# Down projection of seven row blocks by a 21-product identity over three token blocks

## The chip, the cores and the metric

The kernel runs on one core of one Trainium2 chip. The metric is the device time of one execution in microseconds, the median of three runs. One execution has a hardware profile: the time of every instruction on each engine. The engines are PE (matmuls), DVE (VectorE, elementwise), ACT (ScalarE, activations and copies), POOL (GpSimd, here only issuing DMAs) and SP (SyncE, issuing DMAs).

## What is computed

One step of a hybrid encoder layer for 384 tokens (256 of a prompt, 128 of running streams), model width 2048: a mixer (pooling branch and state-space branch), and then the MLP, which the change concerns:

```
x1 = x + rmsnorm(mixer output)
h  = square(relu(rmsnorm(x1) @ w_up))      # 384 x 8192
y  = x1 + rmsnorm(h @ w_down)              # w_down: 8192 x 2048
```

All is float32. A float32 product is made of three matmuls on rounded parts: an operand a is split into a high part (rounded to the type fp32r) and a low part (the rest), and a.b is taken as ah.bh + ah.bl + al.bh.

## The kernel before

**The MLP's work.** The 384 tokens are three blocks of 128 (b = 0, 1, 2). The 8192 hidden rows are eight row blocks (c8 = 0 to 7) of 1024 rows, or eight tiles f8 of 128. The 2048 output columns are two halves (p = 0, 1) of 1024 columns, each two blocks of 512. Call a block product the product of 128 tokens x 256 hidden rows x 512 columns: two tiles of rows with three matmuls each, 6 matmuls. Plainly computed, a half of a row block has 3 x 4 x 2 = 24 of them.

An up unit (half a tile f: 8 of the 16 tiles of model width) is 24 matmuls of 384 columns. When a tile's second unit is done, `up_evict` (L1319) takes relu and the norm's factor out of PSUM on DVE (L1322), squares on ACT (L1323), and makes the high part on ACT (L1332) and the low part on DVE (L1333) for the token blocks that are needed plain.

`down_units` (L1359) does a half of a row block for row blocks 0 to 6 in 8 steps of two units each. Token blocks 0 and 1 with the two halves of the row block's rows and the two column blocks go by a 2 x 2 identity of 7 products (r = 0 to 6) of 12 matmuls; token block 2 is computed plainly (r = 7 and 8, 24 matmuls each). That makes 132 matmuls a half. The sums of token blocks are made in `token_sums` (L1307: five DVE sums, one ACT rounding L1316, one DVE subtraction L1317, twice a row block). The sums of weights are DVE additions of 2048 columns (L1367), four a half, each made at the end of the preparation of an earlier step. Each finished product is copied out of PSUM by ACT (L1383) into one of two buffers `ev` and added by a POOL-issued DMA to `acc_scr` in DRAM (L1387; L1385 for the first row block): 9 a half.

The last row block (`last_units`, L1513) is computed plainly, the nine sums per half are loaded back (`begin_last`), `merge` (L1446) makes seven DVE sums a half of them, and the norm and the residual follow.

**Order.** Each engine runs its instructions in the order in which the program issues them. `run` (L1279) walks the list of units: it asks for the weights of the unit 8 later (SP), issues the matmuls of unit i, and prepares unit i + 4: `split4` (L1269) makes the high part of 1024 weight columns on ACT and the low part on DVE (L77 and L78, or L1275 and L1276 for every fourth). There are four pairs of buffers, so ACT's rounding for unit i + 4 waits for the matmuls of unit i. A unit's `post` (relu and so on for an up unit, eviction for a down unit) comes ahead of that preparation for an up unit and behind it for a down unit. The list alternates two down units and one up unit of the next row block (L1578 to L1582).

Of the kernel before, what the change touches and what calls it, by code (L numbers as in the profile page):

```python
# [7 lines left out]
F32 = mybir.dt.float32  # L8
# [25 lines left out]
V_GPRE, V_GMLP, V_PSC, V_CW, V_CB, V_NRM, V_DSK, V_DTB, V_ALOG, V_END = 0, 16, 32, 48, 240, 288, 320, 352, 353, 384  # L34


def build(ctx, tc, io):
# [963 lines left out]
    acc_scr = [[dram.tile([P, 512], F32, name=f"acc_scr{p}_{i}") for i in range(9)] for p in range(2)]  # L1001
# [258 lines left out]
    t8 = pg.tile([P, 8, T], F32, name="t8")  # L1260
    sf = pg.tile([P, 4, 2, P], F32, name="sf")
    sh = pg.tile([P, 4, 4, P], F32R, name="sh")
    sl = pg.tile([P, 4, 4, P], F32R, name="sl")
    raws = ExitStack()
    pr = raws.enter_context(tc.tile_pool(name="phr", bufs=4, reuse_waits="tile"))
# [13 lines left out]
    def run(units, far=8):  # L1279
        n = len(units)  # L1280
        got, hl = [None] * n, [None] * n

        def fetch(i):
            if i < n and units[i][0]:
                got[i] = units[i][0]()

        def prep(i):
            if i < n:
                hl[i] = units[i][1](got[i])

        for i in range(far):
            fetch(i)
        for i in range(DEPTH):
            prep(i)
        for i, (_, _, mm, post, soon) in enumerate(units):
            fetch(i + far)
            mm(hl[i])
            if soon:
                post()
            prep(i + DEPTH)  # L1300
            if not soon:
                post()
            hl[i] = got[i] = None

    nothing = lambda *_: None

    def token_sums(k):  # L1307
        a11, a12 = t8[:, k, :P], t8[:, 4 + k.start : 4 + k.stop, :P]
        a21, a22 = t8[:, k, P:TP], t8[:, 4 + k.start : 4 + k.stop, P:TP]
        f = [sf[:, i, :, :] for i in range(4)]  # L1310
        v.tensor_tensor(f[0], a22, a21, ALU.subtract)
        v.tensor_tensor(f[3], a11, a12, ALU.subtract)
        v.tensor_tensor(f[3], f[3], f[0], ALU.add)
        v.tensor_tensor(f[2], a11, a21, ALU.subtract)
        v.scalar_tensor_tensor(out=f[1], in0=f[0], scalar=-1.0, in1=a11, op0=ALU.mult, op1=ALU.subtract)
        s.activation(sh[:, :, k, :], sf, AF.Copy)  # L1316
        v.tensor_tensor(sl[:, :, k, :], sf, sh[:, :, k, :].bitcast(F32), ALU.subtract)  # L1317

    def up_evict(f, ps):  # L1319
        f8 = f % 8  # L1320
        t = t8[:, f8, :]
        v.scalar_tensor_tensor(out=t, in0=ps, scalar=0.0, in1=r2, op0=ALU.max, op1=ALU.mult)  # L1322
        s.activation(t, t, AF.Square)  # L1323
        blocks = range(3) if f8 >= 4 else (0, 2)
        n = len(blocks)
        tag = f"{f8}_{f // 8 % 2}"
        h = pg.tile([P, n, P], F32R, tag=f"hh{tag}", name=f"hh{f}")
        l = pg.tile([P, n, P], F32R, tag=f"hl{tag}", name=f"hl{f}")
        tb = t.rearrange("p (b t) -> p b t", b=3)
        if n == 2:  # L1330
            tb = tb[:, 0:3:2, :]
        s.activation(h, tb, AF.Copy)  # L1332
        v.tensor_tensor(l, tb, h.bitcast(F32), ALU.subtract)  # L1333
        return {b: (h[:, i, :], l[:, i, :]) for i, b in enumerate(blocks)}

    def up_units(c8, hh, skip=0):
        out = []
        for f8 in range(skip, 8):
            f = c8 * 8 + f8
            ps = []  # L1340
            for q in range(2):

                def mm(hl, f=f, q=q, ps=ps):
                    if q == 0:
                        ps.append(mmtile(f"pj_up{f}")[:, :T])
                    half(ps[0], q, hl, xs2)

                def post(f=f, f8=f8, q=q, ps=ps):
                    if q:
                        hh.append(up_evict(f, ps[0]))  # L1350

                out.append(
                    (lambda f=f, q=q: wfetch(io["w_up"][f, q], f"up{f}_{q}"), lambda w: split4(*w), mm, post, True)
                )
        return out

    NAMES = ("11", "12", "22", "21")

    def down_units(c8, p, hh):  # L1359
        nm = f"{c8}_{p}"  # L1360
        tok = lambda k0, b: lambda k: hh[k0 + k][b]
        sums = lambda i: lambda k: [sh[:, i, k, :], sl[:, i, k, :]]
        raw, t2 = {}, []
        src = {n: io["w_down"][c8, p, i] for i, n in enumerate(NAMES)}

        def add(d, n):
            v.tensor_tensor(raw[d], raw[d], raw[n], ALU.add)  # L1367

        steps = [
            ("11", True, [(0, tok(0, 0)), (7, tok(0, 2))], nothing),  # L1370
            ("12", True, [(8, tok(0, 2))], lambda: add("11", "12")),
            ("21", True, [(1, tok(4, 0)), (7, tok(4, 2))], nothing),
            ("22", True, [(2, sums(3)), (8, tok(4, 2))], lambda: add("12", "22")),
            ("11", False, [(4, sums(0))], lambda: add("22", "11")),
            ("12", False, [(6, sums(2))], lambda: add("21", "22")),
            ("22", False, [(5, sums(1))], nothing),
            ("21", False, [(3, tok(4, 1))], nothing),
        ]
        begins, ends = {7: 0, 8: 1}, {7: 2, 8: 3}

        def evict(r, o):
            e = pg.tile([P, 512], F32, tag="ev", name=f"ev{nm}_{r}", bufs=2)
            s.copy(e, o)  # L1383
            if c8 == 0:
                gp.dma_start(acc_scr[p][r], e)  # L1385
            else:
                gp.dma_start(acc_scr[p][r], e, accum_op=ALU.add)  # L1387

        out = []
        for j, (kd, load, uses, then) in enumerate(steps):  # L1390
            outs = []
            for q in range(2):
                half_cols = slice(q * 1024, q * 1024 + 1024)

                def fetch(kd=kd, q=q, hc=half_cols):
                    if q == 0:
                        raw[kd] = pr.tile([P, 2048], F32, tag="raw", name=f"raw{nm}_{kd}")
                    sy.dma_start(raw[kd][:, hc], src[kd][:, hc])

                def prep(_, j=j, q=q, kd=kd, hc=half_cols, then=then):  # L1400
                    hl = split4(raw[kd][:, hc], f"wd{nm}_{j}_{q}")
                    if q:
                        then()
                    return hl

                def mm(hl, j=j, q=q, uses=uses, outs=outs):
                    if j == 0 and q == 0:
                        t2.extend(sstile(f"t2_{nm}_{i}") for i in range(2))
                    if q == 0:
                        outs += [t2[r - 7] if r >= 7 else mmtile(f"wd{nm}_{r}") for r, _ in uses]  # L1410
                    wh, wl = hl
                    for k2 in range(2):
                        k = q * 2 + k2
                        c = slice(k2 * 512, k2 * 512 + 512)
                        for (r, a), o in zip(uses, outs):
                            ah, al = a(k)
                            first = k == 0 and (r < 7 or begins[r] == j)
                            fin = k == 3 and (r < 7 or ends[r] == j)
                            te.matmul(o, ah, wh[:, c], start=first, stop=False)  # L1419
                            te.matmul(o, ah, wl[:, c], start=False, stop=False)  # L1420
                            te.matmul(o, al, wh[:, c], start=False, stop=fin)  # L1421

                def post(j=j, q=q, uses=uses, outs=outs):
                    if q == 0:
                        return
                    for (r, _), o in zip(uses, outs):
                        if r < 7 or ends[r] == j:
                            evict(r, o)
                    if p == 0 and j < 2:
                        token_sums(slice(2 * j, 2 * j + 2))  # L1430

                out.append((fetch if load else None, prep, mm, post, False))
        return out

    c8 = NC - 1
    ac, hacc, tail = [], [], {}

    def begin_last():
        raws.close()
        fin = ctx.enter_context(tc.tile_pool(name="fin", bufs=1, reuse_waits="tile"))  # L1440
        for p in range(2):
            ac.append([fin.tile([P, 512], F32, name=f"ac{p}_{i}") for i in range(9)])
            for i in range(9):
                gp.dma_start(ac[p][i], acc_scr[p][i])

    def merge(p):  # L1446
        a1, a2, a3, a4, a5, a6, a7 = ac[p][:7]
        v.tensor_tensor(a2, a1, a2, ALU.add)
# [122 lines left out]
    def first_mm(hl, mm=mm):  # L1571
        mm(hl)
        norm2()
        for i in range(2):
            hh0.append(up_evict(i, ps_up[i]))
# [143 lines left out]
```

## Time and profile before

| what | value |
|---|---|
| median of 3 runs | 2796.72 us (2796.18 to 2797.13) |
| span of the profiled execution | 2795.4 us (the page gives no other time of it) |
| PE busy | 2783.4 us |
| DVE busy | 1766.9 us |
| ACT busy | 1323.8 us |
| granted clock of PE, mean | 0.999 |

The span is the time from the first to the last instruction. Matmuls are pipelined, so that the durations of single ones overlap; their cadence is read from their starts. "Idle before" a group is the time that the engine stood still ahead of it, with what it waited for.

### The profile page before, as it was taken

The numbers are of one execution on the slowest core, as the hardware profiler recorded it, in microseconds if no ns is written. First come the engines' busy times: TensorE is split into PE (matmuls) and PEld (weight loads), VectorE is DVE, ScalarE is ACT, GpSimd is POOL, SyncE is SP. The second block draws the span as 40 slices with busy tenths as digits, with TensorE's granted clock in tenths as the row PEclk, the third lists the DMA queues.
The fourth block names the chain that finished last, engine by engine and source line by source line (L and its number), as shares of the span: only waits on it lengthen the run. The fifth ranks groups of instructions, "written<-read, shape, count | busy, mean of one in ns | idle before, by whom it ended". The sixth has DMA issues, their size and how long they took to land.

```text
span 2795.4 us, 40257 instructions
## 1 busy us (share of the span) xinstructions
PE 2783.4 (100%) x15964; PEld 2654.1 (95%) x15964; DVE 1766.9 (63%) x2217; ACT 1323.8 (47%) x2076; POOL 191.0 (7%) x295
## 2 busy tenths in 40 slices
PE   9999999999999999999999999999999999999998
PEld 9999999999999999999999988999999999999997
DVE  8774334567767767667643333666767667676766
ACT  6443223555555555554422223545555555555553
POOL 0000000000000000001000000000111111111111
PEclk9999999999999999999999999999999999999999
DMA  6444445556556556555744454445666566666656
GB/s 223 135 134 139 137 141 172 190 171 216 196 179 211 196 183 206 200 182 187 263 154 159 148 201 135 159 164 185 178 159 166 162 161 163 179 178 185 181 128 247
DMA packets 161468, 492.89 MB, mean 176 GB/s; under 512 B 20032, under 2 KB 43392, under 8 KB 156416
## 3 DMA queue, kind: packets, MB, share of 16 engines
q1 hardware_dynamic: 133008, 406.07, 43.4%
q0 software_dynamic: 28128, 84.24, 12.6%
q8 instruction: 125, 2.05, 0.3%
q14 instruction: 63, 0.52, 0.1%
q10 hardware_dynamic: 144, 0.01, 0.0%
HBM read 412.35 MB, written 77.89 MB: 175 GB/s over the span
## 4 chain that ended last, share of the span: by engine, by line
PE 90%; DVE 4%; issue 2%; ACT 2%; DMA 1%; SPq 0%; POOL 0%; DVEq 0%; ACTq 0%; POOLq 0%
PE pj_up L162 6%; PE pj_up L163 6%; PE pj_up L164 6%; PE pj_x L164 3%; PE pj_x L162 3%; PE pj_x L163 3%; PE wd L1419 3%; PE pj_sp L163 3%; PE wd L1421 3%; PE wd L1420 3%; PE pj_sp L164 3%; PE pj_sp L162 3%; PE pj_z L162 2%; PE pj_z L163 2%; PE pj_z L164 2%
## 5 line engine op out<-in xcount | busy, mean ns | idle before, releaser
L162 PE MATMUL pj_up<-x1h,wh_up 128*128 128x384 f32 x992 | 334.2, 337 | 0.0
L163 PE MATMUL pj_up<-x1l,wh_up 128*128 128x384 f32 x992 | 333.3, 336 | 0.0
L164 PE MATMUL pj_up<-x1h,wl_up 128*128 128x384 f32 x992 | 333.3, 336 | 0.0
L162 PE MATMUL pj_x<-xgh,wh_x 128*128 128x384 f32 x768 | 257.2, 335 | 0.0
L164 PE MATMUL pj_x<-xgh,wl_x 128*128 128x384 f32 x768 | 256.6, 334 | 0.0
L163 PE MATMUL pj_x<-xgl,wh_x 128*128 128x384 f32 x768 | 256.6, 334 | 0.0
L78 DVE TENSOR_TENSOR wl_wd<-raw,wh_wd 128x1024 fp32r<-128x1024 f32 x168 | 201.9, 1223 | 62.7 <-ACT wh_wd L77 61.2
L77 ACT ACTIVATE wh_wd<-raw 128x1024 fp32r<-128x1024 f32 x168 | 174.2, 1053 | 84.5 <-PE pj_up L163 42.1
L162 PEld LDWEIGHTS pj_up<-x1h,wh_up 128*128 128x128 f32 x992 | 186.5, 188 | 4.5
L163 PEld LDWEIGHTS pj_up<-x1l,wh_up 128*128 128x128 f32 x992 | 186.5, 188 | 4.5
L164 PEld LDWEIGHTS pj_up<-x1h,wl_up 128*128 128x128 f32 x992 | 186.5, 188 | 0.0
L164 PE MATMUL pj_z<-xgh,wl_z 128*128 128x384 f32 x512 | 171.1, 334 | 0.0
L162 PE MATMUL pj_z<-xgh,wh_z 128*128 128x384 f32 x512 | 171.1, 334 | 0.0
L163 PE MATMUL pj_z<-xgl,wh_z 128*128 128x384 f32 x512 | 171.1, 334 | 0.0
L162 PE MATMUL pj_sp<-abh,wh_sp 128*128 128x384 f32 x512 | 171.0, 334 | 0.0
L163 PE MATMUL pj_sp<-abl,wh_sp 128*128 128x384 f32 x512 | 171.0, 334 | 0.0
L164 PE MATMUL pj_sp<-abh,wl_sp 128*128 128x384 f32 x512 | 171.0, 334 | 0.0
L78 DVE TENSOR_TENSOR wl_sp<-w_sp,wh_sp 128x1024 fp32r<-128x1024 f32 x64 | 78.4, 1225 | 110.7 <-ACT wh_sp L77 110.7
L162 PEld LDWEIGHTS pj_x<-xgh,wh_x 128*128 128x128 f32 x768 | 144.2, 188 | 0.0
L163 PEld LDWEIGHTS pj_x<-xgl,wh_x 128*128 128x128 f32 x768 | 144.2, 188 | 0.0
L164 PEld LDWEIGHTS pj_x<-xgh,wl_x 128*128 128x128 f32 x768 | 144.2, 188 | 0.0
L78 DVE TENSOR_TENSOR wl_x<-w_x,wh_x 128x1024 fp32r<-128x1024 f32 x72 | 87.5, 1222 | 81.3 <-ACT wh_x L77 81.3
(392 smaller groups left out, 7087.3 us busy)
## 6 DMA issues: line engine op xcount, KB each, us to landing
w_up<-w_up SPq DMA_DIRECT2D x126, 512.0 KB, 4.5
raw<-w_down SPq DMA_DIRECT2D x112, 512.0 KB, 7.2
w_x<-w_in SPq DMA_DIRECT2D x96, 512.0 KB, 4.2
w_z<-w_in SPq DMA_DIRECT2D x64, 512.0 KB, 4.6
w_sp<-w_ssd SPq DMA_DIRECT2D x64, 512.0 KB, 5.0
acc_scr<-ev POOLq DMA_DIRECT2D x126, 256.0 KB, 4.4
w_ga<-w_in SPq DMA_DIRECT2D x32, 512.0 KB, 3.5
w_pp<-w_pp SPq DMA_DIRECT2D x32, 512.0 KB, 3.4
```

Source lines behind the costliest of these rows:

```text
L77: s.activation(h, w, AF.Copy)
L78: v.tensor_tensor(l, w, h.bitcast(F32), ALU.subtract)
L162: te.matmul(out, wh, xh, start=first, stop=False)
L163: te.matmul(out, wh, xl, start=False, stop=False)
L164: return te.matmul(out, wl, xh, start=False, stop=last)
L1419: te.matmul(o, ah, wh[:, c], start=first, stop=False)
L1420: te.matmul(o, ah, wl[:, c], start=False, stop=False)
L1421: te.matmul(o, al, wh[:, c], start=False, stop=fin)
```

## The change

Seven row blocks' down products are now made by one bilinear identity over all three token blocks, the four pairs of row tiles and the two column blocks: 21 block products a half, 6 matmuls each. It has three tables. `A_FORMS` says how 21 token forms are made from the 12 blocks of h (three token blocks by four pairs of tiles) with 20 sums of 256 columns: 14 forms need one sum, 3 need two, 4 need none. Every form is then rounded on ACT and subtracted on DVE. `B_UNITS` lists 15 units a half: the sums of weight blocks (1024 columns) made first, the buffer that is split, the blocks loaded, and the products (form, bank). `C_OPS` lists 14 sums a half that make six output blocks of the 12 banks at the end.

```
+B_UNITS = [([], 0, [(5, 0)], [(0, 0), (1, 1)]), ([(0, 1, -1, 0, 1)], 0, [(7, 1)], [(2, 1)]),
+ ([(2, 1, -1, 2, 1)], 2, [(3, 2)], [(3, 2)]), ([(2, 3, 1, 2, -1), (1, 2, 1, 1, -1)], 1, [(2, 3)], [(4, 3), (5, 0)]),
+ ([], 3, [], [(6, 4), (7, 5)]), ([(4, 0, 1, 4, 1)], 4, [(1, 4)], [(8, 2), (9, 5)]),
+ ([(4, 5, 1, 4, -1), (0, 0, 1, 4, 1)], 0, [(0, 5)], [(10, 3)]), ([], 5, [], [(11, 4)]), ([], 2, [], [(12, 6)]),
+ ([(0, 2, -1, 4, 1)], 0, [], [(13, 7)]), ([(2, 3, -1, 2, 1)], 2, [(6, 3)], [(14, 8)]), ([], 3, [], [(15, 9)]),
+ ([(3, 3, -1, 6, 1), (3, 4, 1, 3, 1)], 3, [(4, 6)], [(16, 8), (17, 10)]), ([], 6, [], [(18, 10), (19, 9)]),
+ ([], 4, [], [(20, 11)])]
+NBUF, NSTAGE, NC_, LOOK = 7, 5, 12, 5
```

In what follows d0 to d14 are these units of a half: d1, d2, d5, d9 and d10 make one weight sum, d3, d6 and d12 two; d0, d3, d4, d5, d12 and d13 have two products, the others one.

The sums stand directly ahead of the split in a unit's preparation, and the forms are made in a new step at the end of each iteration of `run`, three at most, of those whose old content has been multiplied for the last time in half 1 of the row block before (`freed`):

```
             if not soon:
                 post()
+            if forms:
+                forms_step()
...
+    def form(c, r, ops, src, sign):
+        for d, x, sx, y, sy in ops:
+            signed_sum(part(c, d), part(c, x), sx, part(c, y), sy)
+        a, h, l = part(c, src), fh[r], fl[r]
+        s.activation(h, a, AF.Copy, scale=float(sign))
+        if sign > 0:
+            v.tensor_tensor(l, a, h.bitcast(F32), ALU.subtract)
+        else:
+            v.scalar_tensor_tensor(out=l, in0=a, scalar=-1.0, in1=h.bitcast(F32), op0=ALU.mult, op1=ALU.subtract)
+
+    def forms_step():
+        for _ in range(3):
+            if forms and forms[0][1] < freed[0] and (forms[0][0], forms[0][2]) in hid:
+                c, r, _, ops, src, sign = forms.popleft()
+                form(c, r, ops, src, sign)
...
+            def prep(_, ops=ops, b=b, g=g):
+                raw_load(g + LOOK)
+                for d, x, sx, y, sy_ in ops:
+                    signed_sum(raw[d], raw[x], sx, raw[y], sy_)
+                return split4(raw[b], f"wd{g}")
...
+            def post(prods=prods, u=u):
+                if p and u == 0:
+                    forms_begin(c8 + 1)
+                for r, c in prods:
+                    if p:
+                        freed[0] = r + 1
+                    if c_last[c] == r:
+                        e = pg.tile([P, 512], F32, tag="ev", name=f"ev{c8}_{p}_{c}", bufs=2)
+                        s.copy(e, bank[c])
```

`signed_sum` is one DVE instruction. `up_evict` keeps only relu and square; the results stay in seven `hid` tiles of two row tiles each. PSUM is divided into 2 banks for up units and 6 for down units instead of 4 and 4. Weight blocks go into seven fixed buffers, asked for on SP in the preparation of the unit five earlier. Twelve banks a half instead of nine are evicted to `acc_scr`; the twelve of half 0 are loaded back after the last up unit, those of half 1 with the last row block.

Up units run ahead: 24 come first (12 more than before), then the halves take 4 and 12 up units among their 15 down units, the last two row blocks 4 and 8, and 2 and 6:

```
+    def spread(downs, ups):
+        out, n = [], 0
+        for u, d in enumerate(downs):
+            while n < len(ups) and (n + 0.5) * len(downs) <= u * len(ups):
+                out.append(ups[n])
+                n += 1
+            out.append(d)
+        return out + ups[n:]
...
+            n = (4, 12)[p] if c < NC - 3 else {0: 4, 1: 8, 2: 2, 3: 6}[(c - NC + 3) * 2 + p]
+            units += spread(down_units(c, p), take(min(n, left)))
```

The forms of the first row block are made three an iteration from the twelfth up unit on, with nothing to wait for. Those of the last row block are plain roundings of the 12 blocks.

More of the change, by code (lines that the diff above doesn't have):

```diff
@@ L1000, in build @@
     x1_scr = dram.tile([P, 3, DM], F32, name="x1_scr")
-    acc_scr = [[dram.tile([P, 512], F32, name=f"acc_scr{p}_{i}") for i in range(9)] for p in range(2)]
+    acc_scr = [[dram.tile([P, 512], F32, name=f"acc_scr{p}_{i}") for i in range(12)] for p in range(2)]
     def wo_open():
@@ L1302, in run, with signed_sum @@
                 post()
+            if forms:
+                forms_step()
             hl[i] = got[i] = None
[L1305 to L1317, printed above, removed]
+    def signed_sum(d, x, sx, y, sy):
+        if sx > 0:
+            v.tensor_tensor(d, x, y, ALU.add if sy > 0 else ALU.subtract)
+        elif sy > 0:
+            v.tensor_tensor(d, y, x, ALU.subtract)
+        else:
+            v.scalar_tensor_tensor(out=d, in0=x, scalar=-1.0, in1=y, op0=ALU.mult, op1=ALU.subtract)
@@ new lines, in build, with part @@
+    forms, freed = deque(), [len(A_FORMS)]
+    def part(c, q):
+        return stage[q[1]] if q[0] == "s" else hid[c, q[1] % 4][:, :, q[1] // 4 * P : q[1] // 4 * P + P]
+    def form(c, r, ops, src, sign):
[5 more added lines that the diff above has]
+            v.tensor_tensor(l, a, h.bitcast(F32), ALU.subtract)
+        else:
+            v.scalar_tensor_tensor(out=l, in0=a, scalar=-1.0, in1=h.bitcast(F32), op0=ALU.mult, op1=ALU.subtract)
@@ L1319, in up_evict, with forms_begin @@
+    def forms_step():
[3 more added lines that the diff above has]
+                form(c, r, ops, src, sign)
+    def forms_begin(c):
+        freed[0] = 0
+        if c < NC - 1:
+            forms.extend((c, r, 3, *a) for r, a in enumerate(A_FORMS))
+        else:
+            forms.extend((c, n, n // 3, [], ("t", n % 3 * 4 + n // 3), 1) for n in range(12))
     def up_evict(f, ps):
-        f8 = f % 8
@@ L1328, in up_evict @@
[L1328 to L1354, printed above, removed]
-        return out
@@ L1357, in build @@
[L1357 to L1411, printed above, removed]
-                    for k2 in range(2):
[L1413 to L1432, printed above, removed]
-        return out
@@ L1435, in build @@
[L1435 to L1448, printed above, removed]
-        v.tensor_tensor(a6, a1, a6, ALU.add)
-        v.tensor_tensor(a7, a6, a7, ALU.add)
-        v.tensor_tensor(a4, a7, a4, ALU.add)
-        v.scalar_tensor_tensor(out=a7, in0=a7, scalar=-1.0, in1=a5, op0=ALU.mult, op1=ALU.subtract)
-        v.tensor_tensor(a6, a6, a5, ALU.add)
-        v.scalar_tensor_tensor(out=a3, in0=a6, scalar=-1.0, in1=a3, op0=ALU.mult, op1=ALU.subtract)
@@ L1456, in enter_last, with up_units, mm, post @@
-    def enter_last():
+        if k2:
+            hid[c, i] = hid["open"]
+    def up_units(f):
+        out, ps = [], []
+        for q in range(2):
+            def mm(hl, q=q):
+                if q == 0:
+                    ps.append(mmtile(f"pj_up{f}")[:, :T])
+                half(ps[0], q, hl, xs2)
+            def post(q=q):
+                if q:
+                    up_evict(f, ps[0])
+                    if f == 8 * NC - 1:
+                        ups_done()
+            out.append((lambda q=q: wfetch(io["w_up"][f, q], f"up{f}_{q}"), lambda w: split4(*w), mm, post, True))
+        return out
@@ L1564, in last_units @@
         return out
-    hh0 = []
-    hs_ = [hh0] + [[] for _ in range(NC - 1)]
-    units = up_units(0, hs_[0], 2)
+    def spread(downs, ups):
[6 more added lines that the diff above has]
+        return out + ups[n:]
+    ups = [x for f in range(2, 8 * NC) for x in up_units(f)]
+    take = lambda n: [ups.pop(0) for _ in range(n)]
+    units = take(12)
+    start = units[-1][3]
+    units[-1] = (*units[-1][:3], lambda: (start(), forms_begin(0), freed.__setitem__(0, 99)), True)
     fetch, prep, mm, post, soon = units[0]
@@ L1677 @@
         "w_up": _tiles(np, a["w_up"][0], range(0, 4 * DM, P)),
[L1678 removed]
+        "w_down": _grouped(np, a["w_down"][0][: 7 * 1024]),
         "w_dlast": _moving(np, a["w_down"][0][7 * 1024 :]),
```

139 lines of the change are left out of this document (97 added, 42 removed), and 11 rows, old and new, of the table A_FORMS.

## The prediction

> **What bounds the kernel now.** I read the page's engine shares first, then the clock row and the chain.
>
> ```profile
> PE 2783.4 (100%) x15964; PEld 2654.1 (95%) x15964; DVE 1766.9 (63%) x2217; ACT 1323.8 (47%) x2076; POOL 191.0 (7%) x295
> ...
> PEclk9999999999999999999999999999999999999999
> ...
> PE 90%; DVE 4%; issue 2%; ACT 2%; DMA 1%; SPq 0%; POOL 0%; DVEq 0%; ACTq 0%; POOLq 0%
> ```
>
> PE never rests, at full clock, and is 90% of the chain. The stage that changes, read by the windows view in its middle, says the same: 120 of 120 us on PE, 84 on DVE (VectorE), 64 on ACT (ScalarE), so DVE has some 30% to spare.
>
> ```profile
> 2180.00:2300.00 120.00, 120.00 (x615) 110.11 (x614) 84.37 (x82) 64.16 (x80) 13.74 (x16) 1.00 0.65 174
> ```
>
> The groups by line and shape count the down matmuls, and the rows of the tile wd say when they begin and when the last row block's begin.
>
> ```profile
> L1419 PE MATMUL wd<-wh_wd,sh 128*128 128x512 f32 x224 | 87.2, 390 | 0.0
> L1419 PE MATMUL t<-wh_wd,hh 128*128 128x512 f32 x224 | 87.2, 389 | 0.0
> ...
> L1419 PE MATMUL wd<-wh_wd,hh 128*128 128x512 f32 x168 | 65.4, 390 | 0.0
> ...
> L1419 PE MATMUL wd<-wh_wd,hh x168: 389/389/391, 1835.1 to 2715.8; 128*128 128x512 f32 x168
> ...
> L1524 PE MATMUL wd<-wh_wd,hh x80: 389/389/391, 2720.7 to 2785.3; 128*128 128x512 f32 x80
> ```
>
> 616 of each of three kinds are 1848 matmuls, 132 for each of 14 halves (seven row blocks, p = 0 and 1). A block product is 6 matmuls, so a half has 22 of them now, not 24. Seven row blocks take 2720.7 - 1835.1 = 885.6 us, 126.5 each. The 389 ns overlap; the cadence and the hand-overs stand in the timeline:
>
> ```profile
> 2060.60 0.39 PE L1419 MATMUL wd<-wh_wd,sh 128*128 128x512 f32 x1
> ...
> 2060.80 0.56 DVE L1322 SCALAR_TENSOR_TENSOR t<-pj_up,r 128x384 f32<-128x384 f32 x1 [1.23 <-PE pj_up L164]
> ...
> 2061.39 0.53 ACT L1323 ACTIVATE t<-t 128x384 f32<-128x384 f32 x1 [2.73 <-DVE t L1322]
> ...
> 2062.38 1.05 ACT L77 ACTIVATE wh_wd<-raw 128x1024 fp32r<-128x1024 f32 x1
> ...
> 2063.32 0.34 PE L162 MATMUL pj_up<-x1h,wh_up 128*128 128x384 f32 x1
> ...
> 2063.46 1.22 DVE L78 TENSOR_TENSOR wl_wd<-raw,wh_wd 128x1024 fp32r<-128x1024 f32 x1 [0.39 <-ACT wh_wd L77]
> ...
> 2064.60 1.22 DVE L1276 TENSOR_TENSOR wl_wd<-raw,wh_wd 128x1024 fp32r<-128x1024 f32 x1
> ...
> 2065.74 2.28 DVE L1367 TENSOR_TENSOR raw<-raw,raw 128x2048 f32<-128x2048 f32 x1
> ...
> 2067.49 0.39 PE L1419 MATMUL wd<-wh_wd,sh 128*128 128x512 f32 x1
> ```
>
> Twelve down matmuls lie between 2060.60 and 2063.32: 0.227 us each. The 24 of an up unit (call it U) run to 2067.49: 4.17 us. The order of DVE and ACT is that of the program: each stands still at its next instruction until that can go. Back to back, a 1.22 us subtraction starts the next after 1.14.
>
> **PE's part.** 21 products are 126 matmuls a half, 6 fewer; 14 x 6 x 0.227 = 19.0 us saved. A row block then needs 252 x 0.227 + 16 x 4.17 = 123.8 us of PE: half 0, with 4 U, 45.2; half 1, with 12 U, 78.6.
>
> **DVE's and ACT's part.** These rows price the new steps:
>
> ```profile
> L78 DVE TENSOR_TENSOR wl_wd<-raw,wh_wd 128x1024 fp32r<-128x1024 f32 x168 | 201.9, 1223 | 62.7 <-ACT wh_wd L77 61.2 <-DMA w_up<-w_up 1.4
> L1367 DVE TENSOR_TENSOR raw<-raw,raw 128x2048 f32<-128x2048 f32 x56 | 127.9, 2284 | 0.0
> ...
> L1333 DVE TENSOR_TENSOR hl<-t,hh 128x256 fp32r<-128x256 f32 x32 | 13.6, 425 | 33.3 <-ACT hh L1332 33.3
> ...
> L1312 DVE TENSOR_TENSOR sf<-t 128x256 f32<-128x256 f32 x14 | 5.9, 418 | 0.0
> ...
> L1317 DVE TENSOR_TENSOR sl<-sf,sh 128x1024 fp32r<-128x1024 f32 x14 | 17.2, 1226 | 15.8 <-ACT sh L1316 15.8
> ...
> L1316 ACT ACTIVATE sh<-sf 128x1024 fp32r<-128x1024 f32 x14 | 14.9, 1061 | 48.3 <-DVE sf L1315 48.3
> ...
> L1332 ACT ACTIVATE hh<-t 128x256 fp32r<-128x256 f32 x32 | 13.4, 418 | 1.0
> ...
> L1383 ACT COPY ev<-wd 128x512 f32<-128x512 f32 x98 | 55.4, 565 | 0.0
> ```
>
> L1317 is the pattern that the change multiplies: DVE makes a sum, ACT rounds it, DVE subtracts. DVE idles 15.8 / 14 = 1.13 us for an ACT of 1.06, so the two hand-overs cost 0.07. Now this happens twice a row block. The weight sums at L1367 do not have it: they are made well before their split. After the change a sum stands directly ahead of the split of the same tile, in 8 of the 15 units of a half, and 17 of the 21 token forms are sum, rounding, subtraction.
>
> Costs on DVE's queue, from one start to the next. A sum 1024 wide has no row: half of L1367's 2.28 is the lower bound, L78's 1.22 the upper; I take 1.22 where ACT waits for its end. So a unit with one sum takes 1.22 + 0.07 + 1.05 + 1.14 = 3.48, with two 4.62, without 1.14. A form with one sum: 0.42 + 0.07 + 0.42 + 0.34 = 1.25, with two 1.59, without 0.34. A relu (L1322) back to back 0.48. Where forms stand ahead of a unit without sum, ACT begins that unit's rounding only behind the last form's: 1.75 instead of 1.14. Where a relu stands ahead of one, the Square of 0.53 and the rounding of 1.05 come after it: 0.48 + 1.63 + 1.14 = 3.25.
>
> I put half 1 in the order that the diff writes (d0 U d1 U d2 d3 U d4 U d5 U d6 U d7 d8 U d9 U d10 U d11 U d12 d13 U d14 U); each iteration prepares the unit four later and then makes the forms just freed. Of its 27 preparations 10 are plain (11.4), 4 stand behind forms (7.0), 4 behind a relu (13.0), 6 have one sum (20.9), 3 have two (13.9); the other 2 relus take 1.0; the forms take 14 x 1.25 + 3 x 1.59 + 4 x 0.34 = 23.7. That is 90.9 us against PE's 78.6. Only some 61 of it is DVE at work (39 splits and sums and 6 relus, 41 short form steps, at their back-to-back prices); 30 is DVE waiting for ACT. Half 0 comes to 12 x 1.14 + 4 x 3.48 + 3 x 4.62 + 2 x 0.48 + 0.8 (ACT busy with an eviction) = 43.3, under PE's 45.2; but DVE may be only four units ahead, and at its end (d12, d13, U, d14, d0, U) it waits for PE: I take 47.0. A row block: 137.9 instead of 126.5.
>
> What stands behind these waits: while DVE stands at a subtraction, the next unit's sum and a U's relu stand behind it, and PE waits for the subtraction. While ACT stands at a rounding whose sum is not made, the eviction copies and the forms' roundings stand behind it; POOL's accumulation waits for the copies, and PE's bank only five units later.
>
> Against PE's own time these are the terms. Five steady row blocks at 137.9 - 123.8 = 14.1 each: +70.5 (bounds 8 each, if most of the roundings queued behind forms and Squares are hidden after all, and 20, if no step overlaps the next by its 0.08 and landings of evictions come on top). The sixth, whose half 1 has 8 U: 4 plain, 9 behind forms, 1 behind a relu, 5 with one sum, 4 with two, 3 relus and the forms make 84.6; with half 0 131.6 against PE's 45.2 + 28.6 + 33.4 = 107.2: +24 (15 to 30). The seventh: half 0 with 2 U takes 10 x 1.14 + 5 x 3.48 + 2 x 4.62 + 2.5 = 40.5 against 36.9, its half 1, with 12 forms without sums, some 50 under PE's 53.6: +5 (2 to 10). The first row block's forms, 3 an iteration behind 7 U: 44 us of queue beside 29 of PE, less 8 that is prepared ahead: +7 (0 to 10). PE's saving: -19.0. Together +87.5.
>
> What I cost at nothing: evictions rise from 9 to 12 a half with two buffers, and two fall together at d5 and at d13, so ACT can stand for a landing. Weights and the last stage's merge have these rows beside them:
>
> ```profile
> acc_scr<-ev POOLq DMA_DIRECT2D x126, 256.0 KB, 4.4
> ...
> raw<-w_down SPq DMA_DIRECT2D x112, 512.0 KB, 7.2
> ...
> L1448 DVE TENSOR_TENSOR ac<-ac,ac 128x512 f32<-128x512 f32 x2 | 1.4, 684 | 0.0
> ```
>
> The evictions hide in half 0 behind PE, else they cost up to 2 us a half. Weights are asked for five units ahead, 8 us or more against 7.2; SP stands behind the sums' release of a buffer, which four units of prepared work cover. The last stage gets 14 more merge sums, 9 us, in two column blocks of 16.3 us of PE; the prepared units cover it, else 2 us. PSUM banks come round after five units or more: nothing.
>
> A rule that speaks against the change: the Trainium skill, TensorE: Matmul & The Clock Gate, section "Why this matters for your kernels", warns that a rest of PE over some 3 us drops its clock to half. By it the third rival below would come true; by the clock row, full in all 40 slices, the sum stands. No run here shows which, since PE never rests in this stage. What a low clock costs in this kernel only its first matmuls show, 631 ns where a warm one of this width has 389:
>
> ```profile
> L313 PE MATMUL warm_o<-warm 128*128 128x512 bf16 x9 | 4.0, 631 | 1.2 <-DVE warm L302 1.2
> ```
>
> **Rivals.** First, PE stays the bound: 2796.7 - 19.0 = 2777.7, faster. For it speak DVE's 30% to spare and the four prepared units; against it L1317's idle. It decides if the waiting in half 1 stays under 78.6 - 61 = 17.6 us where I count 30. Second, part is hidden: if the 9 us of roundings that queue behind forms and Squares in half 1 vanish (4 x 0.61 + 4 x 1.63), a steady row block takes 129 and the sum is 5 x 5.2 + 17 + 5 + 4 - 19 = +33: 2830. Third, PE's clock falls in its rests: my order leaves PE rests of up to 4 us in half 1 (before d6). One fall in each of the six halves 1 that are long, with 4 us of work at 631 for 389 ns, is 6 x 2.5 = 15; where half 0 then starts late as much again at most. I put 25: 2909.
>
> **How the numbers follow.** The forecast has 0.58, the clock 0.08, the part hidden 0.14, PE as the bound 0.17, something close to no change 0.03. Predicted: 2796.7 + 87.5 = 2884. The span of the profile, 2795.4, is 1.3 below the median; both move alike. The terms' lower bounds give 2796.7 + 40 + 15 + 2 + 0 - 19 = 2835, the upper ones 2796.7 + 100 + 30 + 10 + 10 - 19 = 2928. The range reaches down over the part hidden, to 2808, and up to 2935; it leaves out PE as the bound and no change, 0.2. Faster by over 0.2% (5.6 us, about what a measurement here can tell): 0.17; within it 0.03; slower 0.80.
>
> **What would show it.** Right: 1764 down matmuls, PE some 4% idle and only in this stage, its waits released by the low parts (L78's successor), most in the halves with forms; DVE's idle put down to ACT's roundings and no longer to PE's up matmuls, some 40 us of it a row block; a steady row block of 138 us. Each form with a sum shows one DVE idle of some 0.5 us. Wrong: PE at 100% and 123.8 us a row block (first rival); PEclk below 9 in slices of this stage (third); ACT waiting for evictions' landings, or DVE for weights (what I cost at nothing).

## The result and the profile after

| | before | after |
|---|---|---|
| median | 2796.93 us (2796.18 to 2798.19, 4 runs) | 2972.57 us (2969.39 to 2974.99, 4 runs) |
| ratio | | 1.0629, 95% interval 1.0613 to 1.0644 |
| span of the profiled execution | 2795.4 us | 2967.6 us |
| granted clock of PE, mean | 0.999 | 0.981 |

The change costs 176 us, twice the 87.5 of the forecast and outside its range. The page of after, its engine shares, its clock row and its chain by engine:

```profile
PE 2840.4 (96%) x15880; PEld 2668.6 (90%) x15880; DVE 1856.5 (63%) x2465; ACT 1341.7 (45%) x2184; POOL 228.4 (8%) x343
...
PEclk9999999999999999999999999999999999999898
...
PE 58%; issue 21%; DVE 8%; ACT 5%; DMA 4%; POOL 3%; SPq 0%; POOLq 0%; ACTq 0%; DVEq 0%
```

PE now rests 4% of the span, and the chain, 90% PE before, goes through DVE, ACT, DMA and POOL. DVE and ACT are as far from full as before (63% and 45% of the span), so neither bounds the kernel by its work. The rows of the tile wd (least, median and most of a matmul's duration, then the first and the last start):

```profile
L1436 PE MATMUL wd<-wh_wd,fh x588: 387/389/797, 1888.8 to 2879.8; 128*128 128x512 f32 x196
...
L1552 PE MATMUL wd<-wh_wl,fh x96: 387/389/628, 2880.5 to 2957.5; 128*128 128x512 f32 x96
```

588 of each of three kinds are 1764 down matmuls, as they should be, and they begin at 1888.8. A longest duration of 797 ns beside a median of 389 says that some ran at half the clock. What PE waited for between 1888.8 and 2880.5 (total, times, longest):

```profile
PE wd L1436 <- ACT wh_wd L104: 43.7, 22, 3.4
PE wd L1437 <- DVE wl_wd L105: 24.1, 36, 0.8
PE pj_up L189 <- ACT wh_up L104: 11.7, 9, 3.1
PE wd L1436 <- ACT wh_wd L1303: 9.7, 7, 2.5
```

These are the prepared weights, high parts from ACT ahead of low parts from DVE: PE is starved, not stopped by its PSUM. And what DVE and ACT waited for from 1820 to 2900:

```profile
DVE wl_wd L105 <- ACT wh_wd L104: 148.7, 123, 4.2
ACT ev L1448 <- DMA acc_scr<-ev: 121.4, 49, 6.1
ACT fh L1352 <- DVE stage L1337: 113.1, 88, 2.1
...
ACT wh_wd L104 <- DVE raw L1337: 93.1, 34, 4.0
```

The first, third and fourth are the hand-overs of the forecast: sum on DVE, rounding on ACT, subtraction on DVE. The second is not: 121.4 us in which ACT stands at an eviction's copy until an earlier eviction has landed in DRAM. The forecast had it at nothing.

Taking every 42nd start of L1436 cuts the stage into its 14 halves. In us, after:

| row block | 0 | 1 | 2 | 3 | 4 | 5 (sixth) | 6 (seventh) |
|---|---|---|---|---|---|---|---|
| half 0 | 48.7 | 59.2 | 60.6 | 58.9 | 59.9 | 58.8 | 54.8 |
| half 1 | 88.4 | 89.4 | 89.8 | 90.9 | 89.4 | 80.8 | 62.0 |

Half 1 came out near the forecast (90.9), half 0 did not (47.0). One row block in the windows view (PE, PEld, DVE, ACT and POOL busy, granted clock, DMA share, GB/s):

```profile
2026.00:2085.00 59.00, 51.58 (x223) 43.08 (x222) 40.71 (x40) 28.33 (x37) 9.68 (x12) 0.91 0.60 158
2085.00:2174.60 89.60, 83.61 (x417) 76.09 (x416) 59.31 (x78) 41.55 (x62) 10.27 (x12) 0.96 0.58 154
```

In half 0 DVE works 40.71 of 59.00 us and ACT 28.33. One reason, which the first experiment tests, is in ACT's timeline within that half (start, duration, idle before in brackets), with the landing of an eviction from the DMA issues below it (KB, median us from issue to landing):

```profile
2055.48 0.57 ACT L1448 COPY ev<-wd 128x512 f32<-128x512 f32 x1
2058.01 0.59 ACT L1448 COPY ev<-wd 128x512 f32<-128x512 f32 x1 [1.97 <-DMA acc_scr<-ev]
...
2068.83 0.59 ACT L1448 COPY ev<-wd 128x512 f32<-128x512 f32 x1 [1.97 <-DMA acc_scr<-ev]
...
2074.14 0.59 ACT L1448 COPY ev<-wd 128x512 f32<-128x512 f32 x1 [2.35 <-DMA acc_scr<-ev]
```

```profile
acc_scr<-ev POOLq DMA_DIRECT2D x168, 256.0 KB, 4.8
```

With two buffers, a copy can go only when the eviction before last has landed: 4.8 us behind its issue. While ACT stands there, the next unit's rounding stands behind it, and DVE's subtraction behind that. The landings of the last two rows are waited for by 1.97 and 2.35 us, in a half that was to hide them.

The last stage is longer too: from its first matmul to the end it takes 2967.6 - 2880.5 = 87.1 us, before 2795.4 - 2720.7 = 74.7. DVE's timeline there:

```profile
2902.65 6.71 DVE L1491 TENSOR_TENSOR ac<-ac,ac 128x512 f32<-128x512 f32 x11 [1.45 <-DMA ac<-acc_scr]
2909.28 1.22 DVE L1304 TENSOR_TENSOR wl_wl<-w_wl,wh_wl 128x1024 fp32r<-128x1024 f32 x1
...
2921.31 1.23 DVE L105 TENSOR_TENSOR wl_wl<-w_wl,wh_wl 128x1024 fp32r<-128x1024 f32 x1 [4.86 <-ACT wh_wl L104]
2922.45 8.76 DVE L1491 TENSOR_TENSOR ac<-ac,ac 128x512 f32<-128x512 f32 x14
```

The merge sums (L1491) are issued in one piece ahead of the next subtraction of weights (L1304), which therefore waits 6.71 and 8.76 us for them, and PE for that, 5.2 us at the longest (2880 to 2967):

```profile
PE wd L1553 <- DVE wl_wl L1304: 8.4, 2, 5.2
```

### The profile page after: what moved, and what is told of

It is laid out like the page before. It is cut to its first block, busy times and chain, and to the rows that moved or that the text cites. A ratio compares the mean times of both kernels' runs of the same rounds, so it can differ in the third digit from the quotient of the medians.

```text
span 2967.6 us, 40646 instructions
## 1 busy us (share of the span) xinstructions
PE 2840.4 (96%) x15880; PEld 2668.6 (90%) x15880; DVE 1856.5 (63%) x2465; ACT 1341.7 (45%) x2184; POOL 228.4 (8%) x343
## 4 chain that ended last, share of the span: by engine, by line
PE 58%; issue 21%; DVE 8%; ACT 5%; DMA 4%; POOL 3%; SPq 0%; POOLq 0%; ACTq 0%; DVEq 0%
PE pj_x L190 3%; PE pj_x L191 3%; PE pj_x L189 3%; POOL acc_scr L1452 3%; PE pj_sp L191 3%; PE pj_sp L190 3%; PE pj_sp L189 3%; PE pj_z L189 3%; PE pj_z L190 3%; PE pj_z L191 3%; DMA acc_scr<-ev 2%; PE pj_pp L189 2%; PE pj_ga L189 2%; PE pj_ga L190 1%; PE pj_ga L191 1%
## 5 line engine op out<-in xcount | busy, mean ns | idle before, releaser
L189 PE MATMUL pj_up<-x1h,wh_up 128*128 128x384 f32 x992 | 341.7, 344 | 15.0 <-ACT wh_up L104 11.7
L191 PE MATMUL pj_up<-x1h,wl_up 128*128 128x384 f32 x992 | 341.0, 344 | 7.5 <-DVE wl_up L105 6.6
L1436 PE MATMUL wd<-wh_wd,fh 128*128 128x512 f32 x588 | 242.4, 412 | 53.4 <-ACT wh_wd L104 43.7
L105 DVE TENSOR_TENSOR wl_wd<-raw,wh_wd 128x1024 fp32r<-128x1024 f32 x157 | 191.4, 1224 | 148.8 <-ACT wh_wd L104 148.7
L1437 PE MATMUL wd<-wl_wd,fh 128*128 128x512 f32 x588 | 246.5, 419 | 30.5 <-DVE wl_wd L105 24.1
L104 ACT ACTIVATE wh_wd<-raw 128x1024 fp32r<-128x1024 f32 x157 | 164.7, 1055 | 173.2 <-DVE raw L1337 93.1
L1438 PE MATMUL wd<-wh_wd,fl 128*128 128x512 f32 x588 | 239.9, 408 | 0.0
L1436 PEld LDWEIGHTS wd<-wh_wd,fh 128*128 128x128 f32 x588 | 116.1, 197 | 87.4 <-ACT wh_wd L104 54.3
L1452 POOL DMA_DIRECT2D acc_scr<-ev x144 | 123.3, 871 | 726.4 <-ACT ev L1448 713.3
L1437 PEld LDWEIGHTS wd<-wl_wd,fh 128*128 128x128 f32 x588 | 116.4, 198 | 68.3 <-DVE wl_wd L105 38.4
```

The lines of the kernel that those rows point to most:

```text
L104: s.activation(h, w, AF.Copy)
L105: v.tensor_tensor(l, w, h.bitcast(F32), ALU.subtract)
L189: te.matmul(out, wh, xh, start=first, stop=False)
L191: return te.matmul(out, wl, xh, start=False, stop=last)
L1436: te.matmul(o, ah, wh[:, cols], start=c_first[c] == r and k2 == 0, stop=False)
L1437: te.matmul(o, ah, wl[:, cols], start=False, stop=False)
```

## The experiments

**Theories.** The working theory: the order of the instructions on DVE and ACT, sum, rounding, subtraction one behind another, together with two eviction buffers, starves PE; with the same instructions in another order PE would bound, and the saved matmuls would show. The rivals: PE's falls to half the clock are what makes half 0 long; or DVE and ACT simply have more work than fits beside PE.

**More eviction buffers.** Five instead of two; nothing else.

```
-  e = pg.tile([P, 512], F32, tag="ev", name=f"ev{c8}_{p}_{c}", bufs=2)
+  e = pg.tile([P, 512], F32, tag="ev", name=f"ev{c8}_{p}_{c}", bufs=5)
```

> The changed kernel with five eviction buffers instead of two. Theory (the accumulating DMAs' landings hold ACT at the eviction copies, 121 us of waits in all, and this is what half 0 lost beyond the forecast): ACT's wait for landings goes to under 10 us; the steady halves 0 fall from 59.5 us to 46 to 49, the steady halves 1 stay at 88 to 91, as the hand-overs between DVE and ACT set them; the time falls by some 75 us to 2885 to 2910. Rival (PE's clock, 0.91 in half 0, makes PE late there): halves 0 stay above 56, the time above 2950. Second rival (loads of weights): no change within 10 us.

Measured: 2927.28 us (2925.24 to 2928.87), ratio to before 1.0467 (1.0451 to 1.0483): 45.3 us less than after. That is less than the 75 us expected, and halves 0 did not come down to the 46 to 49 us expected. ACT no longer waits for a landing. A steady row block in the windows view:

```profile
2024.20:2079.30 55.10, 49.73 (x224) 42.03 (x223) 38.77 (x37) 27.92 (x36) 10.03 (x12) 0.94 0.62 166
2079.30:2166.60 87.30, 81.94 (x415) 74.79 (x414) 61.39 (x82) 41.80 (x63) 10.27 (x12) 0.98 0.59 156
```

Cut in halves as above, halves 0 take 48.8, 55.1, 53.9, 55.0, 55.5, 54.1 and 50.3 us, halves 1 five times 87.3, then 78.2 and 60.9: a gain of 28 us in the seven halves 0 and of 15 in the seven halves 1. The last stage is as long as it was (2924.5 - 2836.4 = 88.1). Most halves 0 are still some 8 us over the forecast. DVE's timeline shows what is left, a unit with one sum:

```profile
2165.50 1.22 DVE L1339 TENSOR_TENSOR raw<-raw,raw 128x1024 f32<-128x1024 f32 x1
2167.93 1.23 DVE L105 TENSOR_TENSOR wl_wd<-raw,wh_wd 128x1024 fp32r<-128x1024 f32 x1 [1.21 <-ACT wh_wd L104]
2169.07 1.22 DVE L105 TENSOR_TENSOR wl_up<-w_up,wh_up 128x1024 fp32r<-128x1024 f32 x1
```

From the sum's start to that of the instruction behind the subtraction 3.57 us, where the forecast had 3.48, with DVE idle for 1.21 in the middle.

**Sums a unit ahead.** The next unit's weight sums are issued between ACT's rounding and DVE's subtraction of this unit, or right behind the subtraction where they would write the buffer that is being split. No instruction is added.

```
+    def sums(g):
+        if g < ntotal and g not in summed:
+            summed.add(g)
+            for d, x, sx, y, sy_ in B_UNITS[g % NU][0]:
+                signed_sum(raw[d], raw[x], sx, raw[y], sy_)
...
-                for d, x, sx, y, sy_ in ops:
-                    signed_sum(raw[d], raw[x], sx, raw[y], sy_)
-                return split4(raw[b], f"wd{g}")
+                sums(g)
+                free = all(o[0] != b for o in B_UNITS[(g + 1) % NU][0])
+                hl = split4(raw[b], f"wd{g}", (lambda: sums(g + 1)) if free else (lambda: None))
+                sums(g + 1)
+                return hl
```

The function handed to `split4` is called in it between the rounding on ACT and the subtraction on DVE.

> The changed kernel with two eviction buffers as it is, but the weight sums of the next unit issued ahead of the subtraction of this one wherever they do not write the buffer that is being split, else right behind it; the same instructions, other order. Theory of the hand-overs: of nine units with sums in a half 1 eight save some 1.2 us each, the steady half 1 falls from 89.5 to about 80; half 0, held by the landings, falls less, to 52 to 57; the time to 2870 to 2900. If the hand-overs do not matter: halves 1 stay above 87, the time above 2950.

Measured: 2893.78 us, ratio 1.0345 (1.033 to 1.0361): 78.8 us less than after. Half 0 takes 46.0 to 54.2 us, a long half 1 83.3 to 86.2, where about 80 was expected. ACT still waits for landings, 142.4 us in all.

**Both.** The two edits above together.

> Five eviction buffers and the sums ahead. Theory: both waits are gone from half 0, which falls to PE's own 45 to 47 us, half 1 to about 80 (forms and roundings still hand over); the time is 2805 to 2830, still above the kernel before. If the two do not add up (one wait hides behind the other): 2850 or more.

Measured: 2828.74 us, ratio 1.0116 (1.0101 to 1.0131): 143.8 us less than after, more than the two alone add up to (124.1): each kind of wait is worth more once the other is gone. A steady row block, and a unit with a sum in DVE's timeline:

```profile
2013.80:2059.60 45.80, 45.57 (x224) 40.22 (x223) 37.19 (x35) 25.08 (x34) 9.53 (x12) 1.00 0.74 202
2059.60:2140.00 80.40, 79.12 (x416) 73.53 (x415) 63.03 (x84) 43.45 (x66) 10.79 (x13) 1.00 0.67 173
```

```profile
2074.85 1.22 DVE L1337 TENSOR_TENSOR raw<-raw,raw 128x1024 f32<-128x1024 f32 x1
2076.48 1.22 DVE L1304 TENSOR_TENSOR wl_wd<-raw,wh_wd 128x1024 fp32r<-128x1024 f32 x1 [0.41 <-ACT wh_wd L1302]
```

The sum now fills the time of ACT's rounding, and 0.41 us of idle is left of 1.21. Half 0 is at PE's own time (45.57 busy of 45.80), the clock 1.00. That DVE and ACT had too much work falls with this: they do the same instructions.

**Forms' low parts later.** On top of both, each form's subtraction is issued behind the next unit's preparation instead of right behind its rounding.

```
-        if sign > 0:
-            v.tensor_tensor(l, a, h.bitcast(F32), ALU.subtract)
...
+        late.append((src, low))
...
+            settle()
```

> As e3, and each token form's subtraction is issued only behind the next unit's preparation (or ahead of a form that overwrites its source). Theory: a good part of the 17 hand-overs of 0.57 us in a half 1 goes too, PE is the bound again in the steady row blocks (123.8 us), the clock stays full; the time is 2780 to 2800, about the kernel before or faster. If DVE's work itself and not the order were the limit: as e3 or slower.

Measured: 2815.48 us, ratio 1.0067 (1.0051 to 1.0084), 13.3 less, and 15 us above the range expected. The steady halves take 45.3 and 78.6 us, which are PE's own 45.2 and 78.6 of the forecast. The first rival of the prediction is true of this kernel's steady row blocks. What is over lies in the sixth (half 1 74.6 for PE's 62.0) and the seventh row block (half 0 46.2 for 36.9) and in the last stage (2813.3 - 2725.8 = 87.5).

**Merge sums spread.** On top of it, two to four merge sums a unit instead of 14 at once, and the load of x1 one column block later.

```
-  if nb < 2 and kp == 1:
-      merge(nb)
+  if nb == 0:
+      merge_some(0, 4 if kp < 3 else 15)
+  elif nb < 3:
+      merge_some(1, 2 if nb * 4 + kp < 11 else 15)
```

> As e4_forms_late, with the merge sums of the last row block issued 2 to 4 a unit instead of 14 at once, and the load of x1 one column block later. Theory (in the last stage DVE stands at the merge sums, first for their loads and then for 14 of them, and the weights' subtractions stand behind: two PE rests of 3.6 and 4.2 us): the last stage falls from 87 us to 76 to 79, the time to 2804 to 2808. Rival (the loads of weights themselves are late, as all loads come at once): under 3 us gained.

Measured: 2809.97 us, ratio 1.0047 (1.0032 to 1.0063), 5.5 less; the last stage takes 2807.7 - 2725.7 = 82.0 us, more than the 76 to 79 expected. The pieces are smaller, but the first waits for its loads:

```profile
2741.48 2.16 DVE L1514 TENSOR_TENSOR ac<-ac,ac 128x512 f32<-128x512 f32 x3 [9.15 <-DMA ac<-acc_scr]
```

DVE stands for 9.15 us until the sums of half 0 are back from DRAM, so spreading the sums was not enough.

**More up units in the late halves.** On top of it, the last two row blocks take 4, 12, 4 and 0 up units instead of 4, 8, 2 and 6, and the twelve sums of half 0 are loaded one a unit in the seventh row block's half 1.

```
-  n = (4, 12)[p] if c < NC - 3 else {0: 4, 1: 8, 2: 2, 3: 6}[(c - NC + 3) * 2 + p]
+  n = (4, 12)[p] if c < NC - 3 else {0: 4, 1: 12, 2: 4, 3: 0}[(c - NC + 3) * 2 + p]
...
+  if p and c8 == NC - 2:
+      ac_one(u)
```

> As e5, with 12, 4 and 0 up units in the last three halves that have them, instead of 8, 2 and 6, and half 0's sums loaded back one a unit in the last half. Theory (a half with fewer up units is set by DVE and ACT: 74.6 and 46.2 us where PE needs 62.0 and 36.9): the sixth row block's half 1 takes 78.6 with four more up units, the seventh's half 0 45.3 with two more, its half 1 without any 38 to 44 instead of 55; together some 10 us less: 2792 to 2800, the kernel before within 0.2% or up to 0.2% faster. If DVE has nothing to give in the steady halves: no gain.

Measured: 2791.46 us (2788.82 to 2795.35, 10 runs) beside 2797.01 of before, ratio 0.9979 (0.997 to 0.9988). This one beats both kernels, the one before by 5.6 us, which is just about what a measurement here can tell; the interval leaves out 1. The engine shares of its page, what PE waited for from 1884 to 2715, and a steady row block and the last stage in the windows view:

```profile
PE 2769.9 (99%) x15880; PEld 2639.6 (95%) x15880; DVE 1851.3 (66%) x2465; ACT 1334.0 (48%) x2184; POOL 228.7 (8%) x343
```

```profile
PE wd L1460 <- DVE wl_wd L1304: 3.9, 5, 1.3
PE wd L1459 <- ACT wh_wd L1302: 2.6, 2, 2.3
```

```profile
2134.00:2258.00 124.00, 124.00 (x639) 114.14 (x639) 99.47 (x118) 68.64 (x99) 20.62 (x25) 1.00 0.72 187
2715.40:2790.40 75.00, 65.46 (x289) 53.89 (x287) 58.95 (x91) 24.45 (x46) 9.70 (x16) 0.95 0.62 224
```

In six row blocks the halves take 45.2 or 45.3 and 78.6 us, 123.9 together, where before has 126.5: the matmuls saved are time saved, once nothing else stands in the way. The last stage is back at 75.0. Against the run before, the halves give 12 us and the last stage 7.0; as the edit changes both the up units and the time of the loads, it does not tell their shares apart. PE is busy for 70.5 us less than in after with the same 15880 instructions. Some 50 of that is the clock: in the granted clock of the traces after spends 116 us at half speed, this kernel 15.8.

**Two eviction buffers again,** in the kernel just shown.

```
-  bufs=5)
+  bufs=2)
```

> As e6_more_ups with two eviction buffers again. If a landing costs time only because ACT has no slack beside the hand-overs, as the prediction's cost of nothing assumed: ACT's waits stay but hide behind PE, the time stays within 6 us of 2791. If two buffers are too few for twelve accumulations in a half 0 of 45 us whatever the order (two buffers turn round in some 6.5 us, so twelve evictions need 39 us and come in bunches): halves 0 grow by 3 us or more, the time goes over 2805.

Measured: 2839.86 us (2833.74 to 2844.2), ratio 1.0148 (1.013 to 1.0165): 48.4 more than with five. What ACT waits for from 1890 to 2840, and a half 0:

```profile
ACT ev L1473 <- DMA acc_scr<-ev: 150.3, 54, 6.6
```

```profile
2011.80:2063.60 51.80, 47.84 (x224) 41.29 (x223) 38.40 (x38) 24.62 (x32) 9.09 (x11) 0.97 0.72 183
```

Two buffers cost 45.3 us in the order of after and 48.4 in the best one: they are too few in both orders tried.

**Evictions without accumulation.** Back to after: each eviction is written to `acc_scr` plainly. This leaves the sums over row blocks out, so only the time is to be read.

```
-  gp.dma_start(acc_scr[p][c], e, accum_op=ALU.add)
+  gp.dma_start(acc_scr[p][c], e)
```

> The changed kernel with two eviction buffers, its evictions written to DRAM without accumulation in all row blocks (the sums over row blocks are left out of the result). If it is the accumulation that makes a landing long: ACT's waits for landings fall from 121 us to under 60 and the time to 2930 to 2950, near e1_five_ev's 2927. If any landing is too long for two buffers: the time stays above 2955.

Measured: 2942.88 us, ratio 1.0528 (1.0511 to 1.0546), 29.7 less than after. ACT's waits, from the same stage, and the landing:

```profile
ACT ev L1448 <- DMA acc_scr<-ev: 59.5, 31, 5.8
...
acc_scr<-ev POOLq DMA_DIRECT2D x168, 256.0 KB, 3.2
```

A plain write lands in 3.2 us, an accumulating one in 4.8; that is 62 of ACT's 121 us. With two buffers even the plain ones hold ACT.

**PE kept busy, twice.** Constant matmuls 128 wide go into columns of the up units' PSUM tile that nothing reads: three for each weight sum, later four, and only while the tile's own sum is open. They change nothing else that is computed.

```
+  for _ in range(3 * len(ops)):
+      te.matmul(hid["ps"][:, T:], ones, ident, start=hid["shut"], stop=hid["shut"])
```

> The changed kernel as it is, with three matmuls of constants, 128 columns wide, into unused PSUM columns ahead of the products of a down unit for each weight sum that the unit makes (33 a half, in row blocks 0 to 5): they only fill rests of PE. Theory (DVE and ACT set the time; PE's lower clock in its rests is a consequence): the clock's low spells shrink from 25 to under 12, the time stays within 15 us of 2972. Rival (the low clock costs a good part of the 88 us beyond the forecast): the time falls by over 25 us.

Measured: 3044.82 us, ratio 1.0878 (1.0859 to 1.0897), 72 more than after. The experiment is flawed:

```profile
PE pj_up L1433 <- DVE hid L1376: 78.5, 29, 7.2
```

From 1890 to 2700 PE's filling matmuls waited 78.5 us for the relu on DVE that reads the other columns of the same tile, a wait that after does not have. The run can't be read for the clock: in its first six halves 0 the clock never fell, and five of them, 58.8 to 60.6 us in after, took 53.7 to 54.8, but the halves 1 ahead of them grew by 15 to 17 us, to 103 to 106. The second form has no such wait, since a tile with its sum open is not yet read:

```
+  if c8 < NC - 2 and not hid["shut"]:
+      for _ in range(4 * len(ops)):
+          te.matmul(hid["ps"][:, T:], ones, ident, start=hid["shut"], stop=hid["shut"])
```

> As e7_fill_rests, but only while an up tile's sum is open in PSUM, where no relu reads that bank and the filling matmuls wait for nothing, four for each weight sum: in half 0 ahead of d2, d3, d10 and d12, in half 1 ahead of d1, d6 and d9. Theory (the low clock is a consequence and hides in DVE's and ACT's time): fewer low spells in half 0, its length within 2 us of 59.5, the time within 12 us of 2972. Rival (the low clock makes halves 0 late): halves 0 fall by 3 us or more, the time by over 15.

Measured: 2972.52 us (2968.36 to 2972.91), ratio 1.0628 (1.0613 to 1.0644): the time of after. The spells at half the clock fell from 25 to 16 and from 116 to 78.5 us in all (counted in the granted clock of the two traces), ACT's waits for landings stayed at 122.4 us. A third less time at the low clock brought no time, but the filling was not free. PE executes 552 instructions more, which take 58 us of it from start to start, while its rests shrank by only 37 us (127.2 to 90.0). So some 21 us came on top, and 38 us less at half the clock give about 19 back. The two cancel, and the run does not decide whether the low clock costs time.

## Why the prediction was wrong

**Right.** The direction, and one part of the mechanism: hand-overs between DVE and ACT hold up the halves, and PE is released by the weights' low and high parts. The counts: 1764 matmuls; PE 4% idle, in part by luck, since matmuls at half the clock count as busy. Half 1, worked out instruction by instruction: 90.9 forecast, 88.4 to 90.9 measured, with DVE at work for 59.31 of 89.60 us in the half shown (forecast 61 of 90.9). That it fits so well is luck too: the measured half holds waits for landings that the forecast had at nothing, and without them, with five buffers, it is 87.3. PE's saving, 19.0: it shows as soon as the waits are gone (123.9 us a row block, forecast 123.8). Loads of weights cost nothing in the halves.

**Where the rest came from.** The terms of the sum beside the spans of after and of the run with five eviction buffers, each cut at the first L1436 matmul of the halves (in us; the forecast's start is 1835.1 + 12 x 4.17 + 7, its last stage that of before):

| part | forecast | after | five buffers |
|---|---|---|---|
| start of the first down matmul | 1892.1 | 1888.8 | 1888.1 |
| five steady row blocks | 689.5 | 735.3 | 704.8 |
| sixth | 131.6 | 139.6 | 132.3 |
| seventh | 94.1 | 116.8 | 111.2 |
| last stage | 74.7 | 87.1 | 88.1 |
| sum | 2882.0 | 2967.6 | 2924.5 |

**The step that failed** is "The evictions hide in half 0 behind PE, else they cost up to 2 us a half." They cost 43 us of the span's 86 beyond the forecast, 3.1 a half, by the last two columns, and 45.3 by the medians. Without them the time is 2927, inside the range of 2808 to 2935. The forecast had the row of the landing (4.4 us) and the two buffers, but did not set the bunch against a buffer's turn. In half 0 six evictions fall due at d5 to d9, two at d5 and one at each of the others, with one U between: by PE's times d8's and d9's come 8.3 and 9.6 us after the first (4.17 + 3 and 4 x 6 x 0.227). Two buffers that come round after a copy of 0.59 and a landing of 4.8 take the fifth no sooner than 2 x 5.4 = 10.8 us after the first: 2.5 late, the size of the waits in ACT's timeline. Four more fall at d12 to d14. And half 0 had no room to hide a wait: it was forecast at 47.0 beside PE's 45.2, with DVE and ACT at 43.3.

**Terms that were too small.** Hand-overs in the steady row blocks: 704.8 for 689.5 with the evictions' waits away, all of it in half 0 (53.7 on average for 47.0, half 1 87.3 for 90.9). A one-sum unit took 3.57 for 3.48; what divides the rest, between dependent sums, DVE's end of the half where it waits for PE, and PE's clock (0.94 in the half 0 shown), stays open. The seventh row block: 111.2 for 94.1, so that "some 50 under PE's 53.6" for its half 1 was too low (60.9, and its half 0 50.3 for 40.5). No experiment took that one apart. It stood 20.7 us above PE's time (90.5); with sums and forms in another order 10.9 of them were left (101.4), and with other up units 12.2 above the PE time of those (86.0 for 73.8). The last stage: "the prepared units cover it, else 2 us" against 12.4. I had the 9 us of sums, but neither that DVE would stand at their loads, nor that a piece of 7 or 9 us holds up every subtraction behind it at once. Spreading the sums took 5.5 us of it away, and the run that loaded half 0's sums earlier, with other up units, 7.0 more (82.0 to 75.0).

**The rivals.** PE as the bound: false of after, where half 1 had the waits that I counted; true of the steady row blocks once sums and forms stood in another order and the evictions had five buffers. Part hidden: false, 149 us a row block and not 129. The clock: the fall that it has did occur, in more places than I counted. Its price stays open. Waits make a half 0 long without it: with sums ahead and two buffers the second and third half 0 have no spell at half the clock and take 49.6 and 50.7 us for PE's 45.2. But a spell seems to cost something there. With five buffers, of the five halves 0 that follow the first, three have two spells of 3.4 us or one twice as long (55.0 to 55.5 us), and two have one (53.9 and 54.1), though PE rests no less in these:

```profile
2166.60:2220.60 54.00, 48.34 (x225) 41.14 (x224) 38.79 (x37) 27.82 (x36) 10.35 (x12) 0.97 0.72 178
```

PE rests 5.66 us here, at a granted clock of 0.97, and 5.37 in the longer half shown with that experiment (55.10 us, 0.94). That is some 1.2 us a spell in halves 0; the five steady halves 1 take 87.3 us, whether they have 3.4 or 6.8 us at half the clock. In after the halves 0 have 61 us at half the clock, so by the same price, an estimate from one trace, some 20 of the 86 us went through the clock; no run takes it out by itself. A spell in half 1 of the row block shown above, in the windows view:

```profile
2099.10:2102.50 3.40, 0.50 (x1) 0.19 (x1) 2.22 (x2) 2.22 (x3) 0.00 (x0) 1.00 0.00 0
2102.50:2105.90 3.40, 3.25 (x8) 2.58 (x9) 2.46 (x5) 1.10 (x3) 0.86 (x1) 0.50 0.44 61
```

The clock was 0.50 for 3.40 us, after 3.40 in which PE had been busy for 0.50.

## What to carry to other kernels

A chain of sum, rounding and subtraction across two in-order engines costs the waits, not the work: issue the next step's first link between this step's links, and the same instructions fit (78.8 us here, 143.8 with the buffers). Set the time in which a buffer comes round (copy, issue, landing) against the closest bunch of its uses, not against their number over a stage. Of the 19 us that 6 of 132 matmuls a half are worth, the best version kept 5.6; 12 went into the one half that had no up units left beside its sums (2715.4 - 2674.7 = 40.7 us for PE's 28.6).

## What the runs showed of the hardware

The clock falls without one long rest. In the spell above PE's two rests were 2.31 and 0.76 us:

```profile
2101.39 0.50 PE L1436 MATMUL wd<-wh_wd,fh 128*128 128x512 f32 x1 [2.31 <-ACT wh_wd L104]
...
2102.65 0.79 PE L1437 MATMUL wd<-wl_wd,fh 128*128 128x512 f32 x1 [0.76 <-DVE wl_wd L105]
```

The Trainium skill, TensorE: Matmul & The Clock Gate, section "Why this matters for your kernels", warns of rests of PE over some 3 us. By that rule this spell would not have come, since neither rest is that long; the measurement differs. What the 25 spells of after have in common is a stretch of 3.4 us before them in which PE was busy for 1.9 us at most; the last of them lies behind the last matmul. Whether that is the condition was not tried.

An accumulating write of 256 KB to DRAM landed 4.8 us behind its issue and a plain one of the same shape 3.2, in two kernels that differ in nothing else (medians of 168; after's hold 24 plain ones of the first row block).
